# One 29,820-instruction program of two transformer blocks, its instruction order taken from another timing model

## The chip, the cores and the metric

One core of a Trainium2 chip runs the whole program. The time is the device time of one execution in microseconds; lower is better. Three executions of the kernel before took 1973.18, 1978.04 and 1979.4 us, so the median is 1978.04 us.

## What is computed

The reference takes 256 tokens of width 1024 through two blocks of two layers each, all in float32.

```
first_block, layer 0:  h = rms_norm(x)*(1+sc1)+sh1;  x += g1 * even_mixer(h)   # 31-tap causal conv + stick-breaking attention
first_block, layer 1:  x += g1 * odd_mixer(h)                                  # 4-tap conv + linear recurrence
both layers:           x += g2 * moe(rms_norm(x)*(1+sc2)+sh2)                   # 16 experts, 2 of 16 for each token
second_block, 2 layers: three attentions (windowed, grouped, low-rank) on x and a 256-token context,
                       then relu(h @ w1)**2 @ w2 with w1 of 1024 x 4096;  layer_norm after each
sh, sc, g:             silu(c) @ mod_w + mod_b, six vectors for each layer and block
```

## The kernel before

Activations lie transposed in SBUF, 128 channels by 256 tokens for each eighth of the width. Float32 matmuls are made of three passes in a rounded format: `split_w` (L327) rounds a 128x1024 weight tile `raw` into `wh` on ScalarE (L333) and takes the rest into `wl` on VectorE (the subtraction in `sub`, L325), and `linear` (L349) runs the three products on TensorE (L345, L346, L347). Weights come by DMA from the SP queue, one 512 KB tile for each `load` (L308), into a ring of buffers; a load waits until the buffer's former tile has been used.

The stages, in order of the program:

- `even_mixer` (L507): projections, the 31-tap convolution `conv` (L514, one tap is L522 on VectorE; for the first quarter of the channels two operations on GpSimd, L519 and L520), `heads` (L554), which normalises q and k by `rstd_of` (L458 to L468: ScalarE Ln, Exp and Square, then three VectorE operations, the first of them L466), and `attention` (L569). Its VectorE convolutions, 90 taps, stand in the program behind the last attention, but read only what was ready long before.
- `mod_steps` (L369): 8 loads and 64 small matmuls (L396) for each modulation vector set. `fill` (L420) lets one such unit into the program between other steps; they are work that nobody waits for yet.
- `moe` (L846): a router, then for each of 16 experts 12 loads of 512 KB whose address the router gives; `up_`, `down` and `combine` (L923, L941, L954). Its ring has 19 buffers. A block that is entered only when an expert has too many tokens follows each of the two `moe` stages; it is not entered here, and the work before and behind it is ordered separately. So there are three long pieces whose order is made each by itself.
- `odd_mixer` (L1008), a second `moe`.
- The second block: `mixer2` (L1249) with `attend` (L1202), which for each 128 x 512 tile of scores takes a maximum on VectorE (L1219), an exponential on ScalarE, a scaling, four transposes on TensorE (L1238) and copies back (L1240), 64 such tiles in layer 0 and 32 in layer 1; then `mlp2` (L1468), a long row of `linear` calls.

Nothing in the source fixes the order of the instructions on an engine. The program is recorded in the order in which the code runs. When the context at the end of `kernel` closes, a scheduler plays the recorded program on a timing model of the core: whenever an engine of the model is free, it gives it, of the instructions whose inputs are there in the model and whose buffers are free in the model, the one that was recorded first. What comes out is one fixed list for each engine, and semaphores are put in where one list waits for another. On the chip every engine then goes through its list in order; an instruction that could run stands still while one ahead of it on the same engine waits. So a step that is recorded late, such as a convolution tap, can stand far ahead in a list, where the model had an engine idle.

## Time and profile before

| | |
|---|---|
| median of three executions | 1978.04 us |
| the profiled execution | 1974.64 us |
| its span, first to last instruction | 1972.9 us |
| TensorE busy | 1788.7 us, 91% |
| VectorE busy | 1092.9 us, 55% |
| ScalarE busy | 736.1 us, 37% |
| GpSimd busy | 125.0 us, 6% |
| moved by DMA | 440.50 MB |
| mean granted TensorE clock | 0.962 |

The shares are means over stages with different limits. The stages lie in the span about so: even mixer 0 to 250 us, first experts 250 to 490, odd mixer 490 to 650, second experts 650 to 890, attention of layer 0 of the second block 890 to 1100, its MLP to 1560, attention of layer 1 to 1715, its MLP to the end.

### The profile page before, as it was taken

How to read it: one execution, taken by the hardware profiler on the slowest of the kernel's cores; microseconds unless marked ns; L12 is line 12 of the kernel's file. 1: busy time of each engine (PE TensorE's matmuls, PEld its weight loads, DVE VectorE, ACT ScalarE, POOL GpSimd, SP SyncE). 2: the span in 40 equal slices, each digit the busy share in tenths (PEclk: the TensorE clock that was granted, in tenths of full speed). 3: DMA queues.
4: the chain of work that ended last, by engine and by line, in shares of the span. 5: the costliest groups of instructions: out<-in, count | busy, mean ns of one | idle time of the engine just before them, and what ended most of it. 6: DMA issues, size and time to landing. Idle time of an engine off the chain costs nothing. (4 is left out here: it accounts for less than half of the span.)

```text
span 1972.9 us, 29820 instructions
## 1 busy us (share of the span) xinstructions
PE 1788.7 (91%) x11134; PEld 1244.2 (63%) x11134; DVE 1092.9 (55%) x2270; ACT 736.1 (37%) x1459; POOL 125.0 (6%) x148
## 2 busy tenths in 40 slices
PE   6799999768799997688999999999999999989997
PEld 3567644212686442126665679888888786569996
DVE  4986502102775121028778567578855767666665
ACT  3345301000483010003667456232323656544443
POOL 0900000000020000001000001000000200010000
PEclk8999999989899998898999999999999999999998
DMA  9566699999765999995111366455644220245551
GB/s 373 186 248 225 248 420 369 420 419 398 289 224 207 419 377 419 420 413 174 53 33 33 127 227 196 161 174 190 187 139 139 93 95 22 68 152 187 183 181 44
DMA packets 122270, 440.50 MB, mean 223 GB/s; under 512 B 13568, under 2 KB 13696, under 8 KB 121856
## 3 DMA queue, kind: packets, MB, share of 16 engines
q1 hardware_dynamic: 122112, 438.46, 60.6%
q8 instruction: 92, 1.51, 0.3%
q14 instruction: 66, 0.54, 0.1%
HBM read 437.35 MB, written 1.05 MB: 222 GB/s over the span
## 5 line engine op out<-in xcount | busy, mean ns | idle before, releaser
L333 ACT CAST wh<-raw 128x1024 fp32r<-128x1024 f32 (+1 forms) x258 | 261.0, 1015 | 282.7 <-PE psL L347 243.2
L325 DVE TENSOR_TENSOR wl<-raw,wh 128x1024 fp32r<-128x1024 f32 (+1 forms) x258 | 309.8, 1203 | 81.1 <-ACT wh L333 80.8
L345 PE MATMUL psL<-h,wh 128*128 128x256 f32 (+1 forms) x800 | 258.6, 323 | 7.8 <-ACT h L341 7.7
L346 PE MATMUL psL<-h,wl 128*128 128x256 f32 (+1 forms) x800 | 257.7, 322 | 2.8 <-DVE wl L325 2.8
L347 PE MATMUL psL<-h,wh 128*128 128x256 f32 (+1 forms) x800 | 255.7, 320 | 0.1
L345 PE MATMUL psL<-gh,wh 128*128 128x256 f32 (+1 forms) x576 | 185.1, 322 | 0.0
L346 PE MATMUL psL<-gh,wl 128*128 128x256 f32 (+1 forms) x576 | 184.6, 321 | 0.0
L917 PE MATMUL psab<-raw,xg 128*32 128x512 f32 (+2 forms) x580 | 142.2, 671 | 34.6 <-DMA raw<-w 26.1
L345 PEld LDWEIGHTS psL<-h,wh 128*128 128x128 f32 x800 | 154.1, 193 | 24.9 <-ACT h L341 8.8
L346 PEld LDWEIGHTS psL<-h,wl 128*128 128x128 f32 x800 | 153.9, 193 | 18.7 <-issue 6.5
L347 PEld LDWEIGHTS psL<-h,wh 128*128 128x128 f32 x800 | 153.6, 192 | 12.7 <-issue 2.5
L933 DVE SCALAR_TENSOR_TENSOR sa<-sa,gs,psab 128x512 f32<-128x512 f32 x14 | 10.5, 748 | 257.8 <-PE psab L917 257.8
L347 PE MATMUL psL<-o,wh 128*128 128x256 f32 (+1 forms) x384 | 120.6, 314 | 0.4
L341 ACT CAST yh<-psY 128x512 fp32r<-128x512 f32 x28 | 16.0, 586 | 280.1 <-PE psY L917 280.1
L345 PEld LDWEIGHTS psL<-gh,wh 128*128 128x128 f32 x576 | 109.5, 190 | 14.5 <-issue 5.8
L346 PEld LDWEIGHTS psL<-gh,wl 128*128 128x128 f32 x576 | 109.6, 190 | 11.1 <-issue 3.7
L917 PEld LDWEIGHTS psab<-raw,xg 128*32 128x32 f32 (+2 forms) x580 | 39.4, 136 | 107.1 <-issue 81.4
L917 PE MATMUL psab<-wh,xg 128*32 128x512 f32 (+2 forms) x212 | 87.2, 722 | 11.9 <-DMA wl<-w 9.0
L917 PE MATMUL psY<-raw,at 128*32 128x512 f32 (+2 forms) x308 | 91.6, 626 | 5.6 <-DMA raw<-w 5.2
L347 PE MATMUL psL<-gl,wh 128*128 128x256 f32 (+1 forms) x288 | 91.9, 319 | 0.0
L917 PE MATMUL psab<-wl,xg 128*32 128x512 f32 (+2 forms) x232 | 80.9, 692 | 11.2 <-DMA raw<-w 5.8
L1085 DVE SCALAR_TENSOR_TENSOR xT<-psL,mod2T,xT 128x256 f32<-128x256 f32 x80 | 38.7, 484 | 90.5 <-PE psL L347 90.3
(459 smaller groups left out, 3622.1 us busy)
## 6 DMA issues: line engine op xcount, KB each, us to landing
raw<-w SPq DMA_DIRECT2D x222, 512.0 KB, 9.9
raw<-fc SPq DMA_DIRECT2D x144, 512.0 KB, 3.4
raw<-mod_w SPq DMA_DIRECT2D x96, 512.0 KB, 6.0
raw<-w_mod SPq DMA_DIRECT2D x96, 512.0 KB, 4.3
wh<-w SPq DMA_DIRECT2D x82, 512.0 KB, 9.9
wl<-w SPq DMA_DIRECT2D x80, 512.0 KB, 9.9
raw<-wo SPq DMA_DIRECT2D x24, 512.0 KB, 4.4
raw<-wi SPq DMA_DIRECT2D x18, 512.0 KB, 3.3
```

The costliest lines, as they stand in the source:

```text
L325: eng.tensor_sub(o, a, hi)
L333: SC.copy(hi[:, :w], raw[:, :w])
L341: SC.copy(hi, src)
L345: T.matmul(o, lhsT=wh, rhs=xh, start=start, stop=False)
L346: T.matmul(o, lhsT=wl, rhs=xh, start=False, stop=False)
L347: T.matmul(o, lhsT=wh, rhs=xl, start=False, stop=stop)
L917: r = T.matmul(o[w * i:w * i + w, :], lhsT=x[:, w * i:w * i + w], rhs=loads[i][0][:, c:c + 512], start=first, stop=last)
L933: V.scalar_tensor_tensor(sa, sa, gs, ob, op0=OP.mult, op1=OP.mult)
L1085: V.scalar_tensor_tensor(src2[s][:, n, :], o[:, s * S:s * S + S], mod2T[l][:, g, s, n:n + 1], src2[s][:, n, :], op0=OP.mult, op1=OP.add)
```

## The change

The context is opened with one more argument. The scheduler, the recorded program, its operations, buffers and waits for data stay the same; the machine that the scheduler plays the program on is another one. The first prices an instruction as one stretch on its engine. The second follows it through separate parts: the sequencer, a stage in which it waits for semaphores, a queue ahead of the engine, the engine, the way of its results out, TensorE's weight loader and clock, and the SBUF ports that VectorE and GpSimd share. Each engine's list may come out in another order, and with it the buffers of a ring that a tile gets and the waits between engines.

```diff
-    with tile.TileContext(nc) as tc:
+    with tile.TileContext(nc, schedule_with_timeline_sim=True) as tc:
         body(tc, aps, out, [_offsets(g) for g in _consts()], _offsets(_params(inputs)))
```

## Rows read from the trace of the kernel before

**Rows 1.** The page: busy time, granted clock and GB/s in forty slices
```profile
PE 1788.7 (91%) x11134; PEld 1244.2 (63%) x11134; DVE 1092.9 (55%) x2270; ACT 736.1 (37%) x1459; POOL 125.0 (6%) x148
...
PEclk8999999989899998898999999999999999999998
...
GB/s 373 186 248 225 248 420 369 420 419 398 289 224 207 419 377 419 420 413 174 53 33 33 127 227 196 161 174 190 187 139 139 93 95 22 68 152 187 183 181 44
```

**Rows 2.** Busy time by stage: stretch, length, engines, clock, DMA share, GB/s
```profile
core 0: us, PE busy (x) PEld busy (x) DVE busy (x) ACT busy (x) POOL busy (x), PEclk, DMA share, GB/s
0.00:35.00 35.00, 17.48 (x155) 6.61 (x155) 10.11 (x63) 8.62 (x20) 0.20 (x4) 0.94 0.96 375
...
61.00:101.00 40.00, 23.74 (x154) 16.91 (x152) 40.00 (x48) 11.38 (x19) 39.14 (x46) 0.85 0.54 189
101.00:200.00 99.00, 95.44 (x748) 71.12 (x749) 70.60 (x175) 54.79 (x117) 1.95 (x3) 0.96 0.70 238
...
250.00:490.00 240.00, 200.27 (x939) 74.31 (x938) 32.87 (x64) 17.23 (x31) 0.00 (x0) 0.94 1.00 406
...
950.00:1100.00 150.00, 147.28 (x715) 88.73 (x708) 115.98 (x354) 102.13 (x268) 8.77 (x12) 1.00 0.09 29
1100.00:1560.00 460.00, 456.15 (x2731) 375.98 (x2727) 312.70 (x504) 175.13 (x290) 16.02 (x12) 1.00 0.53 172
...
1600.00:1715.00 115.00, 110.46 (x644) 76.11 (x644) 81.37 (x219) 69.30 (x166) 5.63 (x12) 1.00 0.13 42
...
1760.00:1950.00 190.00, 188.33 (x1511) 183.15 (x1512) 120.23 (x171) 89.21 (x143) 3.11 (x4) 0.99 0.46 153
```

**Rows 3.** Waits of TensorE over the span: total us, times, longest us
```profile
engine line waited for: us in total, times, longest us
PE psab L917 <- DMA raw<-w: 34.8, 16, 3.1
PE psX L563 <- DVE nr L466: 15.7, 1, 15.7
...
PE psM L396 <- DMA raw<-mod_w: 11.6, 8, 6.7
...
PE psL L345 <- ACT h L341: 7.7, 2, 7.5
```

**Rows 4.** Timeline of TensorE, 84 to 104 us: start, us, instruction, idle before
```profile
84.99 0.28 PE L347 MATMUL psL<-hl,wh 128*128 128x256 f32 x1
...
101.55 1.19 PE L563 MATMUL psX<-sqh,cst 128*128 128x256 f32 x2 [15.72 <-DVE nr L466]
...
103.66 0.58 PE L345 MATMUL psL<-hh,wh 128*128 128x256 f32 x1
```

**Rows 5.** Timeline of ScalarE: the last operation ahead of L466
```profile
81.29 0.42 ACT L465 ACTIVATE nr<-rs 128x256 f32<-128x256 f32 x1
```

**Rows 6.** Timeline of VectorE, 61 to 104 us, convolution taps and L466
```profile
82.12 3.96 DVE L522 SCALAR_TENSOR_TENSOR cv<-u,pv,cv 128x238 f32<-128x238 f32 x5
...
87.62 4.47 DVE L522 SCALAR_TENSOR_TENSOR cv<-u,pv,cv 128x235 f32<-128x235 f32 x6
...
93.63 7.44 DVE L522 SCALAR_TENSOR_TENSOR cv<-u,pv,cv 128x232 f32<-128x232 f32 x10
100.99 0.41 DVE L466 SCALAR_TENSOR_TENSOR nr<-psX,nr 128x256 f32<-128x256 f32 x1
```

**Rows 7.** Busy time of the taps alone (L522) in two stretches
```profile
61.00:100.00 39.00, 28.69 (x38) 0.86 0.55 192
101.00:149.00 48.00, 20.18 (x44) 0.95 0.68 242
```

**Rows 8.** Busy time of GpSimd in the first of them
```profile
61.00:100.00 39.00, 38.14 (x44) 0.86 0.55 192
```

**Rows 9.** Groups of VectorE by line, 950 to 1100 us: busy us, mean ns
```profile
L1219 DVE TENSOR_REDUCE nm<-psS 128x1 f32<-128x512 f32 (+1 forms) x63 | 34.8, 554 | 11.1 <-PE psS L1434 5.6 <-PE psS L347 5.3
...
L1240 DVE COPY pt<-psT 128x256 f32<-128x256 f32 x46 | 18.0, 420 | 11.9 <-PE psT L1238 11.6
```

## The prediction

> **What bounds the kernel now.** I read the page first, then busy time by stage, then TensorE's waits, then the timeline of the one stretch that stood out. TensorE is busy 1788.7 of 1972.9 us [rows 1], so a better order has at most 184 us to give back, and the stages tell how little of that order can reach. In the two expert stages the DMA share is 1.00 [rows 2]: four full slices of each run at 419 to 420 GB/s, or within a few of that [rows 1], whatever TensorE does. TensorE's longest total wait, 34.8 us for expert weights [rows 3], belongs there, and no order of the same bytes shortens it much. In the two MLP stretches of the second block TensorE is busy 456.15 of 460 and 188.33 of 190 us [rows 2]: full. In the attention stretches it is busy 147.28 of 150 and 110.46 of 115 us. The first 35 us are the first weights' arrival at a DMA share of 0.96 [rows 2], with TensorE waiting for them [rows 3]. What is left is one stretch, 61 to 101 us: TensorE busy 23.74 of 40 us while VectorE is busy 40.00 and GpSimd 39.14 [rows 2]. Nearly all of TensorE's idle time there is one wait of 15.7 us, by far the longest of the program [rows 3].
>
> **That wait is one of order.** L563 wants the PSUM buffer that L466 has yet to read. The last input of L466 was finished by ScalarE at 81.29 + 0.42 = 81.71 us [rows 5], and L466 started at 100.99 [rows 6]: 19.28 us in VectorE's list behind work that stood ahead of it, 5, 6 and 10 convolution taps [rows 6] with weight splits between them. The taps are recorded after the attention; they stand there because the first model had VectorE idle. With them the splits are late, the buffers come free late, and the weights of the next projection are late too.
>
> Two things made that list wrong on the chip. One is that the model had the normalisation later against the taps than it came. The other is the price of a tap. From 61 to 100 us 38 taps took 28.69 us, 0.755 us each; from 101 to 149 us 44 took 20.18 us, 0.459 us each [rows 7]. In the first stretch GpSimd worked 38.14 of 39 us [rows 8], in the second it had ended. So the same tap costs 0.296 us more beside GpSimd, together 38 x 0.296 = 11.2 us.
>
> [...]
>
> **The change, part by part.** No operation, byte or buffer is added or removed. The sum is made against the profiled execution, 1974.64 us (span 1972.9, 1.74 around it), and put on the median of the runs, 1978.04, which is 3.4 us higher.
>
> 1. *61 to 101 us.* The second model knows the ports that VectorE and GpSimd share, so in it VectorE is full here, L466 is ready before many of the taps have run, and it goes ahead of them, as it was recorded ahead. The taps go to 101 to 200 us, where VectorE is busy 70.60 of 99 us [rows 2]: 21 taps at 0.459 are 9.6 us into 28 us of room. The ends: 0, if the list stays as it is; 40 - 23.74 = 16.3 us, if TensorE has no idle time left. I take the 11.2 us that the taps cost above their price alone, since the splits' part of VectorE's backlog stays. It is nearer to the upper end because the whole wait has one cause. What is late next is the weight load that waits for a split to free its buffer. Term: -11.2.
>
> 2. *TensorE's clock.* [...] With a shorter hole there are fewer slow matmuls: some ten at 0.3 us, 0 to -3 us. It lies partly inside term 1; I take 0.
>
> 3. *Attention of the second block.* 64 + 32 tiles of scores go through VectorE and ScalarE between two visits to TensorE. TensorE's idle time in both stretches is 2.72 + 4.54 = 7.3 us [rows 2], which is all that a better list can save. A worse list shows one step of a tile, of which the maximum with 0.554 us and the copy with 0.420 us are typical [rows 9]; all 96 tiles at 0.554 are +53 us. Now other tiles and projections hide these steps. The old list hides nearly all of them, and the new one has the same work to hide them with. I take 0, and keep -7 and +53.
>
> 4. *Expert stages.* The loads' order follows the experts, and 19 buffers of 512 KB at 420 GB/s, 1.25 us each, hold 23.7 us of transfers, so a TensorE list that is up to that much out of step costs nothing. The stage moves 406 GB/s [rows 2]; at 420 the 240 us would be 232, so -8 for each stage is the end on the good side. On the bad side 16 waits with 34.8 us [rows 3], 2.2 us each, are the price of a late tile: ten more are +22. Taken: 0.
>
> 5. *MLP stretches.* 3.85 + 1.67 = 5.5 us of TensorE idle time are there at most to gain [rows 2]. The matmuls are recorded in the order in which weights come, so I see no filler that could push in: 0. The start and the end are chains with nothing to reorder: 0.
>
> Sum: -11.2 us; 1974.64 becomes 1963.4 for a profiled execution, and the median 1978.04 becomes 1967.
>
> **The rivals.** *The order hardly changes where it counts: 1978 us.* The second model may set L466 just as late against the taps, because it is the arrival of the first weights that decides when the normalisation can run in the model, or it may move taps and keep as many beside GpSimd. Then term 1 is 0, and changes elsewhere fall where TensorE has other work. For it speaks that the rows show only one wait above 8 us that order made; against it that 19.28 us of standing still is much for a list from a model that counts VectorE's time better. That the lists come out the same in all three pieces belongs here. Chance 0.20, 1972 to 1984 us.
>
> *The attention lists get worse: 2005 us.* A model with a queue ahead of each engine can have an instruction taken into that queue while the engine is still busy. Then matmuls and VectorE steps that are ready early are fixed ahead of a maximum or a transpose that becomes ready a moment later, and on the chip the later one waits. Its place is 950 to 1100 and 1600 to 1715 us, its price 0.554 us for each tile that loses its cover. From 11.2 / 0.554 = 20 of the 96 tiles on it outweighs term 1. With half of the tiles it is 48 x 0.554 = 26.6 us; the same cause would keep taps ahead of L466, so term 1 falls away too: 1978 + 27 = 2005. Against it speaks that TensorE is 98% and 96% busy there, so a list would have to be clearly worse. For it that VectorE, at 115.98 of 150 us, and ScalarE, at 102.13, have little room [rows 2], so that a step put in a wrong place isn't made good at once. Chance 0.32.
>
> *Faster, as in the sum: 1967 us.* Chance 0.48.
>
> **How the numbers follow.** A measurement of this kernel tells about 0.3%, 6 us, from no change. Faster by more than that 0.48, within it 0.20, slower 0.32. The likeliest time is 1967 us. On the good side all gains together are 16.3 + 7.3 + 5.5 + 8 for one expert stage, 37 us: 1941. On the bad side three quarters of the tiles, 72 x 0.554 = 40 us, give 2018. The range is 1941 to 2018. The forecast's own range is 1955 (terms 1 and 3 at their good ends) to 1972.
>
> **What would show it.** Right: in the changed kernel's timeline L466 starts within some 5 us of the ScalarE step ahead of it, the wait of L563 is below 5 us, and from 61 to 101 us there are clearly fewer than 38 taps, with the rest at about 0.46 us each behind GpSimd's end; the expert stages keep their DMA share of 1.00 and about 240 us. Wrong: the wait of L563 is still above 10 us (first rival), or TensorE's idle time from the second block's attention grows from 7 to over 20 us with waits for VectorE and ScalarE steps of `attend` (second), or the DMA share of an expert stage falls below 0.95.

## The result, and the profile after

The changed kernel takes 2026.43 us (four executions, 2020.84 to 2029.34) where the kernel before takes 1978.02 beside it: a ratio of 1.0254, with an interval of 1.0241 to 1.0268. It is 2.5% slower. The prediction said 1967 us, range 1941 to 2018: wrong in sign, and outside the range.

The page of the changed kernel (span 2027.6 us, profiled execution 2029.34), to be read against [rows 1]:

```profile
PE 1808.3 (89%) x11134; PEld 1261.8 (62%) x11134; DVE 1090.3 (54%) x2270; ACT 735.8 (36%) x1459; POOL 127.9 (6%) x148
...
PEclk8987999988789999897989999999999999989998
```

The same 11,134 matmuls keep TensorE busy 19.6 us longer (1808.3 against 1788.7, mean granted clock 0.943 against 0.962), and its idle time grows by 35.1 us (219.3 against 184.2). Together that is the 54.7 us by which the span grew. Every engine has as many instructions as before; VectorE and ScalarE are busy no longer than before, GpSimd 2.9 us longer.

To see where, I cut both traces at the same steps and subtracted: the first `hh` (L504), the last L639, the last `hh` of the odd mixer, the last L646, the last L963, the first and the last L1219, the first L1487. "4 and 1" and the two columns behind it are kernels of the next section; numbers are us.

| stretch | before | after | difference | 4 and 1 | 140 and 48 | 1 and 1 |
|---|---|---|---|---|---|---|
| start to first hh | 34.4 | 38.8 | +4.4 | 38.1 | 38.2 | 38.5 |
| even mixer | 169.2 | 173.1 | +3.9 | 164.9 | 181.6 | 245.2 |
| first experts | 309.9 | 311.7 | +1.8 | 313.4 | 313.7 | 319.9 |
| odd mixer | 85.5 | 104.3 | +18.8 | 82.9 | 107.8 | 96.4 |
| second experts | 288.9 | 292.1 | +3.2 | 290.9 | 293.2 | 300.3 |
| to the first score tile | 64.6 | 70.1 | +5.5 | 67.0 | 63.2 | 82.5 |
| attention, layer 0 | 226.6 | 238.7 | +12.1 | 226.2 | 262.6 | 249.4 |
| MLP of layer 0, attention of layer 1 | 528.9 | 533.0 | +4.1 | 526.1 | 555.6 | 569.6 |
| to the end | 264.9 | 265.8 | +0.9 | 265.5 | 280.8 | 274.5 |

More than half of the loss lies in the odd mixer and in the attention of layer 0. Here is the busy time by stage of the changed kernel (columns as in [rows 2]): 61 to 101 us, the odd mixer, and the attention of layer 0:

```profile
61.00:101.00 40.00, 32.51 (x227) 26.92 (x225) 40.00 (x47) 14.78 (x24) 39.14 (x44) 0.97 0.49 165
...
523.60:627.90 104.30, 88.70 (x681) 80.41 (x683) 60.78 (x105) 55.04 (x108) 17.17 (x16) 0.91 0.46 154
...
990.10:1228.80 238.70, 228.66 (x1347) 154.17 (x1346) 164.58 (x439) 136.68 (x331) 11.79 (x16) 0.97 0.27 89
```

And the same two stages of the kernel before:

```profile
513.50:599.00 85.50, 84.40 (x698) 76.69 (x698) 61.11 (x106) 54.21 (x106) 13.26 (x16) 1.00 0.68 234
...
952.50:1179.10 226.60, 221.53 (x1322) 148.02 (x1324) 158.41 (x433) 133.61 (x325) 12.80 (x16) 0.99 0.28 94
```

The odd mixer was full before: TensorE busy 84.40 of 85.50 us at a clock of 1.00. After, it is idle for 15.6 us, and the clock is 0.91. In the attention of layer 0 idle time goes from 5.1 to 10.0 us, and busy time rises by 7.1 us; part of that rise is 25 more matmuls that fall into this stretch (1347 against 1322).

TensorE's waits in the changed kernel, against [rows 3]:

```profile
PE psab L917 <- DMA raw<-w: 31.7, 14, 3.2
...
PE psL L345 <- ACT cath L341: 13.0, 4, 8.5
...
PE psX L563 <- DVE nr L466: 11.0, 1, 11.0
PE psS L345 <- ACT h L341: 10.8, 5, 5.3
```

The wait for `cath` is new among the long ones. In the kernel before it was

```profile
PE psL L345 <- ACT cath L341: 2.8, 3, 2.0
```

`cath` is the input of the last step of the odd mixer. TensorE's timeline where it stands (start, us, instruction, idle time before it):

```profile
590.89 0.28 PE L347 MATMUL psL<-hl,wh 128*128 128x256 f32 x1
591.10 0.64 PE L396 MATMUL psM<-raw,cond1r 128*32 128x256 f32 x8
593.43 0.61 PE L403 MATMUL psM<-cst,mod_e 128*128 128x8 f32 x4 [1.69 <-ACT mod_e L400]
602.56 0.58 PE L345 MATMUL psL<-cath,wh 128*128 128x256 f32 x1 [8.52 <-ACT cath L341]
602.94 0.41 PE L346 MATMUL psL<-cath,wl 128*128 128x256 f32 x1
```

TensorE has done all the other work of the stage by 594 us, and then stands 8.52 us for ScalarE. A matmul that took 0.28 us ahead of the wait takes 0.41 behind it: here idle time was paid a second time, in slower matmuls. The reason for ScalarE being late lies further up. ScalarE's chain (sigmoid, recurrence, gelu, `cath`) starts with the gate matmuls of L1029 and L1030. They go from 537.4 us on in the kernel before, and from 548.6 in the changed one; start of the first and of the last L1029, before and then after:

```profile
L1029 PE MATMUL psG<-xc,gw x16: 379/379/484, 537.4 to 545.6; 128*128 128x256 f32 x16
```

```profile
L1029 PE MATMUL psG<-xc,gw x16: 377/379/483, 548.6 to 570.6; 128*128 128x256 f32 x16
```

8 us have become 22. In the timeline of the kernel before, two matmuls of the y-projection stand between one pair of gates and the next; in the changed one 48 of the x-projection stand behind the first gates, and then runs of 6 to 24 of the y-projection, 59 in all, and some of the small fillers L396. The y-projection and the fillers are recorded behind the gates and nobody waits for them yet. That is work for TensorE to do while ScalarE runs; the new list does it first.

How far the gates are spread is not the whole of it. Two other lengths make the end of the stage late. One is how far into the stage the last gate starts: 32.5 us in the kernel before, 47.5 in the changed one. The other is the time from there to the first `cath`: 23.5 us before, 31.0 after. The second lies in the lists of the other engines, as 35 and 1 of the next section shows. One part of it can be seen in ScalarE's list: in the changed kernel all eight gelus (`sq`) stand ahead of the first `cath`, in the kernel before it is four. ScalarE, the changed kernel and then the kernel before:

```profile
598.23 2.56 ACT L293 ACTIVATE sq<-sq 128x256 f32<-128x256 f32 x8
...
602.10 2.55 ACT L341 CAST cath<-sq 128x256 fp32r<-128x256 f32 x8
```

```profile
567.21 1.34 ACT L293 ACTIVATE sq<-sq 128x256 f32<-128x256 f32 x4
569.47 1.19 ACT L341 CAST cath<-sq 128x256 fp32r<-128x256 f32 x3 [0.92 <-DVE sq L1053]
```

### The profile page after: what moved, and what is told of

The parts are those of the page before. It is cut to its first block, busy times and chain, and to the rows that moved or that the text cites. A ratio compares the mean times of both kernels' runs of the same rounds, so it can differ in the third digit from the quotient of the medians.

```text
span 2027.6 us, 29832 instructions
## 1 busy us (share of the span) xinstructions
PE 1808.3 (89%) x11134; PEld 1261.8 (62%) x11134; DVE 1090.3 (54%) x2270; ACT 735.8 (36%) x1459; POOL 127.9 (6%) x148
## 5 line engine op out<-in xcount | busy, mean ns | idle before, releaser
L325 DVE TENSOR_TENSOR wl<-raw,wh 128x1024 fp32r<-128x1024 f32 (+1 forms) x258 | 310.2, 1206 | 134.1 <-ACT wh L333 132.5
L917 PE MATMUL psab<-raw,xg 128*32 128x512 f32 (+2 forms) x580 | 143.6, 678 | 33.5 <-DMA raw<-w 23.8
L345 PEld LDWEIGHTS psL<-gh,wh 128*128 128x128 f32 x576 | 109.3, 190 | 12.1 <-issue 3.7
L917 PE MATMUL psY<-raw,at 128*32 128x512 f32 (+2 forms) x308 | 91.5, 603 | 5.6 <-DMA raw<-w 4.7
L345 PE MATMUL psL<-hh,wh 128*128 128x256 f32 x256 | 78.8, 309 | 9.6 <-ACT hh L504 6.2
```

What stands on the lines that cost most here:

```text
L325: eng.tensor_sub(o, a, hi)
L345: T.matmul(o, lhsT=wh, rhs=xh, start=start, stop=False)
L917: r = T.matmul(o[w * i:w * i + w, :], lhsT=x[:, w * i:w * i + w], rhs=loads[i][0][:, c:c + 512], start=first, stop=last)
```

## The experiments

Two theories stood at the start.

*A, early commitment.* The second model has a queue ahead of each engine: by the scheduler's own table 35 instructions for TensorE, 12 for each other engine, counted with the one that is being executed. The scheduler hands a ready instruction to an engine as long as that queue has room, and its place in the list is then fixed. A deep queue is filled with whatever is ready, also with what was recorded late; what is recorded earlier but becomes ready a moment later comes behind all that.

*B, prices.* The second model's durations, ports or transfers put steps in a wrong order, whatever the queue.

The depths are a table of the scheduler, so each can be set ahead of the context, with all else as in the changed kernel (m and n stand for the numbers, and the import is left out):

```diff
 def kernel(**inputs):
...
+    TRN2Spec.ENG_ISSUE_QUEUE_DEPTH = {ET.SP: 12, ET.Activation: n, ET.DVE: n, ET.PE: m, ET.Pool: n}
     arrays = prep(inputs)
```

Below, "35 and 12" is m = 35 and n = 12, the changed kernel. SP's entry is 12, and 1 in the two kernels "1 and 1" and "4 and 1". It makes no difference there: the program built from 4 and 1 with SP at 12 has the same list on every engine.

### All queues, or TensorE's, or all others, at 1

*1 and 1.* 

> The changed kernel, with the second model's queue ahead of each engine cut to one instruction (35 on TensorE, 12 on VectorE, ScalarE and GpSimd in the changed kernel); all of the model's prices stay. Theory A (early commitment: the model takes ready work of later record into an engine's queue while the engine is still busy, so a step that becomes ready a moment later stands behind it in the list): most of the 48 us go, 1965 to 1990 us, and the gate matmuls of the odd mixer (L1029, L1030) come in one run of about 9 us again instead of being spread over 23 us. Theory B (prices: the second model's durations are off for this kernel, and the order is bad for that): the prices are the same, so 2015 to 2040 us.

*1 and 12.* 

> The changed kernel with only TensorE's queue in the model cut from 35 to one instruction. Theory A with TensorE's list as the cause: 1970 to 1995 us. Theory A with the other engines' lists as the cause: about 2015 us. Theory B: 2015 to 2040 us.

*35 and 1.* 

> The changed kernel with the model's queues of VectorE, ScalarE and GpSimd cut from 12 to one instruction and TensorE's left at 35. Theory A with TensorE's list as the cause: 2010 to 2030 us. With the other lists as the cause: 1970 to 1995 us. Theory B: 2015 to 2040 us.

Measured: 2180.0 us for 1 and 1 (1.1057 of the kernel before, 1.1033 to 1.1082), 2191.2 for 1 and 12 (1.1087, 1.1057 to 1.1118), 2015.7 for 35 and 1 (1.0217, 1.02 to 1.0234). Both theories missed the first two by far: TensorE's depth of 1 costs 200 us that neither had. In the third the queues of the other engines are a small part of the whole, some 11 us against 2026.4, but not in the odd mixer. Its odd mixer and the gates in it:

```profile
518.70:605.90 87.20, 83.36 (x664) 75.71 (x667) 59.79 (x105) 53.96 (x105) 15.15 (x16) 0.98 0.55 184
```

```profile
L1029 PE MATMUL psG<-xc,gw x16: 377/379/483, 534.4 to 556.6; 128*128 128x256 f32 x16
```

TensorE's queue is as deep as in the changed kernel, and the gates are spread over 22 us as there. But the last gate starts 38.3 us into the stage, ScalarE's first `cath` comes 21.8 us later, and the stage takes 87.2 us instead of 104.3. The same time from the last gate to the first `cath` is 21.8 to 24.9 us in all kernels with the other queues at 1 and TensorE's at 2 or more, and 29.5 to 31.7 us in all with the other queues at 12 or 48 and TensorE's at 4 or more. So the loss of that stage needs deep queues on both sides. What 35 and 1 loses lies behind it: the attention of layer 0 takes 246.1 us, against 226.6 in the kernel before and 238.7 in the changed one.

### All queues four times as deep

*140 and 48.* 

> The changed kernel with all of the model's queues four times as deep: 140 instructions on TensorE, 48 on VectorE, ScalarE and GpSimd. Theory A: slower again by about as much as the first step cost where ready later work is at hand, 2045 to 2090 us. Theory B: 2015 to 2040 us.

Measured: 2098.6 us (1.0636, 1.0615 to 1.0657), 72 us above the changed kernel. More depth costs more, as A has it, and more than the 2090 us at which its range ended. The wait at the end of the odd mixer grew with it:

```profile
PE psL L345 <- ACT cath L341: 22.0, 4, 17.5
```

### TensorE's queue at 4 and at 12

*4 and 12.* 

> The changed kernel, TensorE's queue in the scheduler's model 4 instructions deep instead of 35 (the other engines keep 12). With 1 the time was 2191 us, with 35 it was 2026, with 140 (and 48 for the others) 2099. Theory A with an overlap price (a queue counts what is executing too, so with 1 the model can overlap neither weight loads nor the ends of matmuls and sees a slow TensorE; beyond what overlap needs, depth only commits too early): with 4 most of the overlap is back and little is committed early: 1975 to 2010 us. Rival (below 35 every loss of depth costs, since the model comes to differ from the chip): 2040 to 2180 us.

*12 and 12.* 

> The changed kernel, TensorE's queue in the scheduler's model 12 instructions deep instead of 35, as the other engines have. Theory A with an overlap price: overlap is whole, a third of the early commitment is left: 1985 to 2015 us. Rival (below 35 every loss of depth costs): 2030 to 2080 us.

Measured: 1989.9 us (1.0079, 1.0062 to 1.0096) and 1999.0 us (1.0122, 1.01 to 1.0143). Both lie where A expected them, and the rival (less depth always costs) is out. The odd mixer takes 86.1 us at 4, 93.0 at 12, 104.3 at 35 and 107.8 at 140; TensorE's idle time in it is 3.1, 8.1, 15.6 and 23.8 us.

### The gates of the odd mixer first

The changed kernel, with one edge for the order on TensorE: the y-projection and its fillers stand behind the last gate.

```diff
-                T.matmul(o[:, S:], lhsT=gw[1][s // 4][:, c], rhs=xc(s), start=True, stop=True)
+                gate = T.matmul(o[:, S:], lhsT=gw[1][s // 4][:, c], rhs=xc(s), start=True, stop=True).ins
...
-                linear(A["od_in"][s], hh, hl, o[:, :S], 0)
+                with tc.issue_after(gate):
+                    linear(A["od_in"][s], hh, hl, o[:, :S], 0)
+                    fill(1)
                 V.tensor_copy(y(s), o[:, :S])
-                fill(1)
```

> The changed kernel with one order edge for TensorE in the odd mixer: the y-projection (the second loop over od_in) and the fillers of that loop may only stand behind the last gate matmul (L1030). Nothing else is held. Theory A (early commitment: the new model's queue ahead of TensorE took later-recorded matmuls in front of gates that became ready a moment later, so that ScalarE's chain of recurrence and gelu starts late and out_proj waits 8.5 us for it): the gates pass in about 9 us as in the kernel before, the waits for cath go, and 10 to 19 of the 54 us come back: 2007 to 2017 us. Rival (the odd mixer is late for another reason, weights or clock, and the place of the gates is only seen beside it): within 5 us of the changed kernel, 2021 to 2031 us.

Measured: 2022.57 us, 1.0251 of the kernel before (1.0233 to 1.0268), so hardly below the changed kernel's 1.0254, and in the range of the rival; but in the profiled execution the odd mixer took 91.5 us instead of 104.3. So both were measured again, beside each other.

*The changed kernel again.* 

> The changed kernel itself, as the reference for the two next runs on the same chip. Its time should stand at 1.025 of the kernel before, as it did: 2020 to 2029 us. No theory speaks against that.

*Gates first, again.* 

> The kernel in which the y-projection of the odd mixer may only stand behind the last gate matmul, once more, beside the changed kernel on one chip. Its one profiled execution had an odd mixer of 91.5 us from the first hh to the last L646 instead of 104.3, but its median was no lower against the kernel before. If the place of the gates is a cause of the loss, it stands 8 to 15 us under the changed kernel, about 2011 to 2018. If what was gained there is given back behind it, or if the 12.8 us were one execution's, it stands within 4 us of it.

Measured: 2029.78 us (1.0267, 1.0249 to 1.0286) and 2023.76 us (1.0246, 1.0228 to 1.0265). The odd mixer, from the trace with the edge, and the gates in it:

```profile
521.60:616.40 94.80, 86.41 (x680) 78.09 (x683) 59.63 (x105) 54.31 (x108) 16.25 (x16) 0.96 0.52 172
```

```profile
L1029 PE MATMUL psG<-xc,gw x16: 377/379/483, 546.5 to 560.4; 128*128 128x256 f32 x16
```

The stage takes 94.8 us against 100.9 beside it (91.5 against 104.3 in the first pair), and in both pairs its idle time halves, from 15.6 to 8.4 and 8.2 us. So the place of the gates is a cause of the loss there, worth 7 us of idle time. Of the whole kernel it gives back 0 to 6 us at the medians, and the intervals overlap: less than the 8 to 15 expected, and not shown to be more than nothing. The edge mends only half of the stage. Between the first gates 48 matmuls of the x-projection still stand, and from the last gate to the first `cath` it is still 29.6 us: the edge leaves the queues of the other engines at 12, and seven gelus still stand ahead of that `cath` in ScalarE's list.

### Term 1 of the prediction by itself

The kernel before, with one edge for the order on VectorE: the taps stand behind the first pair of heads.

```diff
-                    V.scalar_tensor_tensor(d(j), d(j), Pv(gn)[:, 0:1], rs, op0=OP.mult, op1=OP.mult)
+                    r = V.scalar_tensor_tensor(d(j), d(j), Pv(gn)[:, 0:1], rs, op0=OP.mult, op1=OP.mult)
+                    normed.append(r.ins)
...
             for s in range(NP, 4):
-                conv(s, V)
+                with tc.issue_after(normed[1]):
+                    conv(s, V)
```

> The kernel before (first model) with one order edge for VectorE: the 90 convolution taps may only stand behind the last step of the first pair of heads, so none stands ahead of the first two L466. This is term 1 of the prediction by itself. If the term's price was right: 11 us less, with ends 0 and 16: 1962 to 1972 us, and no wait of L563 over 5 us. Rival (the wait is only the first of several at the same time: the next weights, or VectorE's total work up to the end of the mixer, take its place): within 6 us of 1978.

Measured: 1973.55 us beside 1974.5, a ratio of 0.9997 (0.9987 to 1.0007). The hole is gone and no time with it. Busy time by stage, 61 to 101 and 101 to 205 us, with the taps held and then in the kernel before:

```profile
61.00:101.00 40.00, 37.84 (x256) 27.06 (x259) 25.95 (x35) 17.85 (x35) 38.95 (x49) 0.98 0.69 236
101.00:205.00 104.00, 90.14 (x723) 65.54 (x719) 78.67 (x201) 51.65 (x109) 0.00 (x0) 0.92 0.64 218
```

```profile
101.00:205.00 104.00, 99.99 (x788) 74.95 (x791) 73.00 (x182) 57.17 (x122) 1.95 (x3) 0.96 0.70 238
```

TensorE gains 14.1 us of work up to 101 us (37.84 against 23.74, [rows 2]) and loses 9.9 behind it. The new wait stands at the end of the mixer:

```profile
188.74 0.58 PE L345 MATMUL psL<-cath,wh 128*128 128x256 f32 x1 [6.85 <-ACT cath L341]
```

In this kernel the even mixer ends with the chain of taps (the last starts at 174.8 us), normalisation over the convolution, and `cath`. In the kernel before the last tap starts at 149.0 us, and TensorE is busy 99.99 of the 104 us up to the end. TensorE has a fixed amount of work to do until then, and does it early or late. The mixer's end came 1.6 us earlier (202.0 against 203.6).

The taps did become cheaper. Taps alone (L522), 61 to 100, 101 to 149 and 149 to 180 us, with the taps held:

```profile
61.00:100.00 39.00, 5.37 (x7) 1.00 0.70 239
101.00:149.00 48.00, 21.82 (x52) 0.98 0.77 269
149.00:180.00 31.00, 13.56 (x31) 0.97 0.62 203
```

All 90 taps, held and then in the kernel before:

```profile
0.00:180.00 180.00, 40.79 (x90) 0.95 0.77 276
```

```profile
0.00:180.00 180.00, 55.77 (x90) 0.92 0.72 261
```

That is 15.0 us of VectorE's time saved, with next to no effect on the end.

### The early load of cT

The new list issues the 1 MB load of `cT`, which is needed in the second block only, at 17.0 us; the kernel before at 94.6. One edge on the SP queue puts it behind a later load; it then goes at 188.4 us.

```diff
+        loads = []
...
-            SY.dma_start(out=dst, in_=src)
+            loads.append(SY.dma_start(out=dst, in_=src).ins)
...
                 even_mixer()
+                with tc.issue_after(loads[-1]):
+                    SY.dma_start(out=cT, in_=A["cT"])
...
-            SY.dma_start(out=cT, in_=A["cT"])
```

> The changed kernel with one order edge for the SP queue: the 1 MB load of cT, which the new list issues at 17.0 us between the first weights (the kernel before at 94.6 us), may only stand behind a later load of the even mixer. The first hh came at 38.8 us instead of 34.4 in the changed kernel, at every depth of the model's queue (37.9 to 39.1). If the load is the cause, the first hh comes at 34 to 36.5 us (1 MB at 420 GB/s is 2.5 us, the shift seen is 4.4) and the whole takes 0 to 5 us less than the changed kernel. Rival (the order of the small matmuls on TensorE is the cause): first hh at 38 to 39 us.

Measured: 2026.45 us (1.0262, 1.0247 to 1.0278), 3.3 below the changed kernel beside it, within the intervals. Start of the first and last `hh` in that trace (the line is L505 there):

```profile
L505 ACT ACTIVATE hh<-nt,modT x16: 492/508/512, 35.9 to 517.5; 128x256 fp32r<-128x256 f32 x16
```

35.9 us instead of 38.8 and 39.2: the load is two thirds of the 4.4 us lost at the start. It goes at 16.5 to 17.3 us at every depth of the queues: without the edge the first `hh` came at 37.9 to 39.2 us in all kernels with the second model.

### Small queues everywhere

*4 and 1.* 

> The changed kernel with 4 instructions in the model's queue for TensorE and 1 for each other engine. With 4 and 12 it was 1990 us, with 35 and 1 it was 2016, with 35 and 12 it was 2022 to 2026. If the loss is early commitment on every engine, the two gains add up in part: 1976 to 1988 us. Rival (an engine with a queue of 1 can't overlap the end of one instruction with the start of the next in the model, as TensorE couldn't, and that costs as soon as TensorE's own list is good): 1990 to 2020 us.

Measured: 1973.93 us beside 1974.95, 0.9992 (0.9981 to 1.0002). The whole loss is gone, with the same second model, its prices and ports. TensorE is busy 1788.0 us, at a mean clock of 0.96, and the odd mixer takes 82.9 us.

```profile
PE 1788.0 (91%) x11134; PEld 1248.7 (63%) x11134; DVE 1088.8 (55%) x2270; ACT 733.9 (37%) x1459; POOL 131.0 (7%) x148
```

*4 and 1, with the load of cT held.* 

> The second model with 4 instructions in TensorE's queue and 1 in each other, and the load of cT held back behind a later load. With 4 and 1 alone the kernel took 1974 us, 0.999 of the kernel before, with a first hh at 38.1 us; in the changed kernel holding the load brought the first hh from 39 to 35.9. If what is left of the loss is the load, and the rest of the second model costs nothing, this stands 2 to 5 us below the kernel before: 1969 to 1973 us. Rival (the even mixer's end is set by the convolution's chain, as in the kernel with held taps, and takes the gain back): 1973 to 1977 us.

Measured: 1973.84 us beside 1973.34, 1.0001 (0.9992 to 1.0011). The first `hh` came at 35.8 us instead of 38.1, and nothing of it is left at the end, as the rival had it. I found no version that beats the kernel before.

*2 and 1.* 

> The second model with 2 instructions in TensorE's queue and 1 in each other. With 1 and 1 it was 2180 us, with 4 and 1 it was 1974. If what costs 206 us at depth 1 is overlap alone (the queue counts the instruction being executed, so with 1 the model's TensorE can't load weights beside a matmul, looks slower than the chip's and is given hardly any later work), one more place gives most of it back: 1972 to 2000 us. Rival (the time goes down evenly with depth up to 4, for another reason, such as how far ahead the list looks): 2080 to 2140 us.

Measured: 1982.36 us (1.0038, 1.0023 to 1.0053). From 1 to 2 the time falls by 198 us, from 2 to 4 by 8: a jump. Busy time from 40 to 280 us at 1 and 1, and at 2 and 1:

```profile
40.00:280.00 240.00, 172.24 (x1081) 125.26 (x1080) 135.09 (x251) 81.08 (x159) 49.19 (x60) 0.81 0.46 153
```

```profile
40.00:280.00 240.00, 217.45 (x1569) 157.66 (x1569) 161.87 (x369) 97.02 (x203) 55.46 (x62) 0.93 0.70 257
```

With depth 1 TensorE gets 1081 matmuls done there instead of 1569. The count holds the instruction being executed, so at 1 the model can't load weights beside a matmul. On the chip the two overlap: in the changed kernel matmuls are busy for 1808.3 and weight loads for 1261.8 us, together more than the span of 2027.6. The model's TensorE is then slower than the chip's, has no gaps to be filled, and the list comes out nearly as recorded. The jump fits that. The model itself was not traced, so the reason is argued, and only the jump is shown.

All depths together. The last column is a count from the lists of the built programs, over the 5,916 matmul instructions of the third piece (the second block): how many matmuls that were recorded later stand ahead of one in TensorE's list, on the mean. The two columns ahead of it are from the profiled execution.

| TensorE and others | us | ratio to before | odd mixer, us | attention, layer 0, us | later work ahead |
|---|---|---|---|---|---|
| kernel before | 1978.0 | 1 | 85.5 | 226.6 | 3.5 |
| 1 and 1 | 2180.0 | 1.1057 | 96.4 | 249.4 | 1.8 |
| 1 and 12 | 2191.2 | 1.1087 | 98.7 | 252.0 | 1.8 |
| 2 and 1 | 1982.4 | 1.0038 | 83.0 | 233.5 | 4.4 |
| 4 and 1 | 1973.9 | 0.9992 | 82.9 | 226.2 | 4.5 |
| 4 and 12 | 1989.9 | 1.0079 | 86.1 | 226.4 | 5.1 |
| 12 and 12 | 1999.0 | 1.0122 | 93.0 | 228.0 | 5.8 |
| 35 and 1 | 2015.7 | 1.0217 | 87.2 | 246.1 | 6.6 |
| 35 and 12 (the change) | 2026.4 | 1.0254 | 104.3 | 238.7 | 7.2 |
| 140 and 48 | 2098.6 | 1.0636 | 107.8 | 262.6 | 9.3 |

From 4 and 1 on, time and count rise together, in the whole program though not in each stage. Too little later work ahead (1.8) leaves TensorE without cover, too much puts the awaited step behind it. Theory A holds, with the addition for depth 1. B falls as it was put: with small queues the second model's prices cost nothing that can be measured. Whether the prices do harm together with a deep queue, no run shows.

Only the model's depths were varied; no run shows the depth of a queue on the chip. The model's best list came from 4 and 1: a list made as if the queues were short was the better one.

## Why the prediction was wrong, point by point

**What bounds the kernel: right as a reading, wrong as a conclusion.** It counted idle time as what an order can win (184 us at most) and, from full stages, concluded that there was little to lose. A stage at 98% or 99% says that its list is good, not that any list is. The odd mixer, at 84.40 of 85.50 us, was not even in the sum, and lost 18.8 us.

**Term 1, the hole, -11.2 us: the step that failed first.** It failed twice. The hole shrank by 4.7 us only. ScalarE's list, VectorE's and TensorE's in the changed kernel, for the first L466:

```profile
82.83 0.37 ACT L561 COPY q<-psL 128x256 f32<-128x256 f32 x1
96.98 1.04 ACT L333 CAST wh<-raw 128x1024 fp32r<-128x1024 f32 x1 [13.78 <-DVE cv L522]
97.93 0.47 ACT L293 ACTIVATE rs<-psX,epst 128x256 f32<-128x256 f32 x1
...
99.28 0.42 ACT L465 ACTIVATE nr<-rs 128x256 f32<-128x256 f32 x1
```

```profile
93.06 9.12 DVE L522 SCALAR_TENSOR_TENSOR cv<-u,pv,cv 128x246 f32<-128x246 f32 x12
...
105.89 0.41 DVE L466 SCALAR_TENSOR_TENSOR nr<-psX,nr 128x256 f32<-128x256 f32 x1
```

```profile
106.35 1.22 PE L563 MATMUL psX<-sqh,cst 128*128 128x256 f32 x2 [10.98 <-DVE nr L466]
```

L466 now stands 6.2 us behind its input (99.70 to 105.89) instead of 19.3, but the input is late: on ScalarE a weight cast that waits 13.78 us for VectorE stands ahead of the normalisation. The backlog of taps moved from one engine's list to the next. L563 waits 11.0 us instead of 15.7, above the 10 us that the prediction named as the mark of its first rival. And the price was wrong: the kernel with held taps took the hole away entirely and gained 1 us, within its interval. In 4 and 1 the same wait is 14.6 us long and that kernel is as fast as the kernel before:

```profile
PE psX L563 <- DVE nr L466: 14.6, 1, 14.6
```

I priced the longest wait of the program without following the mixer to its end: with the hole gone, another chain ended last there.

**The price of a tap: right.** In the changed kernel 36 taps from 61 to 100 us take 0.763 us each and 51 from 101 to 149 us 0.466, much as in [rows 7]; GpSimd is busy for 38.14 of the first 39 us and for 8.16 of the second 48:

```profile
61.00:100.00 39.00, 27.47 (x36) 0.98 0.51 169
101.00:149.00 48.00, 23.79 (x51) 0.88 0.75 280
```

So in both kernels a tap was slower beside GpSimd. What makes it so on the chip, no run shows: the shared ports that term 1 names are a part of the scheduler's model. What the prediction hung on the price, 11.2 us less for the kernel, did not come: with the taps held, 7 of them from 61 to 100 us instead of 38, VectorE saved 15.0 us over all taps and the kernel nothing.

**Term 2, the clock, 0: mis-sized.** Its 0.3 us for a slow matmul are the 0.58 us behind the hole less the 0.28 ahead of it in [rows 4]. Over the whole program it came to 19.6 us more of busy time for the same matmuls. In the odd mixer the granted clock goes from 1.00 to 0.91 as idle time goes from 1.1 to 15.6 us. I looked at the clock only for the hole that was to go, and not at what new holes would cost.

**Term 3, attention, 0 with -7 and +53: inside the bounds, the wrong value.** Layer 0 lost 12.1 us, 22 tiles' worth at the 0.554 us that I took. The reason for 0, that the new list has the same work to hide the steps with, was the error: the same work hides nothing when it stands ahead of the step that is waited for. The mark of the second rival, over 20 us of TensorE's idle time in the second block's attention, did not come: it is 10.0 us in layer 0, and 3.9 from the first to the last score tile of layer 1.

**Term 4, experts, 0: right.** From 252.4 to 480 us the transfers run at 410 to 423 GB/s in all but the first of forty slices, and the two stages lost 1.8 and 3.2 us. The reading of the kernel before was too high, though: among the full slices of the two stages [rows 1] has one at 369 and one at 377 GB/s. **Term 5, MLP and start, 0: nearly.** The stretches with the MLPs lost 4.1 (with the attention of layer 1) and 0.9 us. The start lost 4.4, which "chains with nothing to reorder" had ruled out: a load that is recorded much later was issued among the first weights.

**The rivals.** "The attention lists get worse" (2005 us, 0.32) named the cause that the runs show, a queue that takes in ready work ahead of a step that becomes ready a moment later. It looked for it in one place, `attend`; the largest loss came in the odd mixer, from the lists of TensorE and of the other engines together, and the stage table of [rows 2] doesn't hold that stage. "The order hardly changes" was right only in its sign, the wait of L563 above 10 us; the time it gave, 1972 to 1984 us, was not.

**In one sum.** The prediction had -11.2 us from 61 to 101 us and nothing elsewhere. The even mixer lost 3.9 us instead, the start 4.4, the odd mixer 18.8, the attention of layer 0 12.1, and the other stretches 15.5 together.

## What to carry to other kernels

When the order of a whole program is made anew, look first at the stages that are full: each can lose, and a stage in which a long chain on another engine starts from a few of TensorE's matmuls loses most (here the odd mixer, 18.8 us) when TensorE's own filler work is put ahead of them, and when the lists of the other engines hold the awaited step back as well. A long wait is worth its length only if nothing that is equally late stands behind it in the same stage; follow the stage to its end before pricing it. If a scheduler plays a queue ahead of the engines, its depth is a parameter of the list to be tried (here 4 and 1 against 35 and 12 was 52 us).

## What the runs showed of the hardware that was not expected

- More idle time of TensorE went with slower matmuls. Over four kernels here, 11,134 matmuls take 1788.0 us at 187.0 us of idle time (4 and 1), 1808.3 at 219.3 (the change), 1823.9 at 272.8 (140 and 48) and 1866.1 at 310.2 (1 and 1): between the first and the last, 78 us of busy time for 123 us of idle time. The relation is not exact: the two executions with the gates first were busy 1797.0 and 1806.3 us at 216.7 and 215.4 us of idle time.
- One 1 MB transfer among the first weights cost about what 1 MB takes at the rate of that time: 2.9 us of delay for the first `hh`, beside 2.5 us for 1 MB (an estimate from the 419 GB/s that the changed kernel's trace shows from 10 to 40 us).
